# Convolution taps summed in a PSUM bank, and a front norm with its GpSimd work taken out or moved, in the second block's mixer

## The chip, the cores and the metric

The kernel runs on one NeuronCore of a Trainium2 chip. The engines are TensorE (PE in the profile), VectorE (DVE), ScalarE (ACT), GpSimd (POOL) and SyncE (SP, which only issues DMAs). The metric is the device time in microseconds, and the median of several runs stands for a kernel.

## The reference, cut to what matters

A network of four layers comes first (two gated units, a recurrence and an attention), then a second block, to which the change belongs. Its mixer computes:

```python
proj = u @ w_in + b_in                       # u: 512 tokens, 1024 features, normed and modulated
q, f, i, og, ca, cgt = split(proj)           # six parts of 512 columns
o = hgrn2(q, f, i)                           # a gated recurrence, 4 heads of 128
h_a = o * rsqrt(mean(o*o)) * norm_w * silu(og)
a = ca * sigmoid(cgt)
a = causal depthwise conv of a, 31 taps for each of the 512 channels, + conv_b
h_b = silu(layernorm(a) * conv_g + conv_bb)
y = concat(h_a, h_b) @ w_out + b_out
```

Behind it stand a residual with a norm, and a mixture of 16 experts of which each token takes two.

## The kernel before, in words

All matrix products are made of three: weights and activations are split into a high half (ScalarE casts, `whi`) and a low half (VectorE subtracts, `wlo`, line 164), and `mm3` (line 171) multiplies high by high, high by low and low by high. A weight block of 128 x 1024 is 24 such matmuls for all 512 tokens. `split()` (line 2838) turns the oldest loaded block into halves and issues the next load; one block is split ahead.

Block 2 (`block2`, line 2811) is issued under a manual schedule: each engine works its instructions strictly in the order in which the program writes them, and waits only for data and for buffers. The names that follow are those of the profile.

- **Front norm**, lines 2854 to 2923. `bn_aggr` gives mean and variance of each token, `col_bcast` (line 275) turns them across into a PSUM bank (`mean`, later `rb`), and `rstd_steps` (line 256) makes the inverse root in 13 small VectorE steps (`ln_x`, `ln_t`, `ln_y`). Before the root, ScalarE copies `mean` to SBUF (`ms`), GpSimd subtracts it from feature chunks 5, 6, 7 (`HSG`, line 2870) and then adds the output bias `b2_gb` to the four token tiles `xtok` (line 2872), which are used only at the end of the block. VectorE subtracts `mean` from chunks 0 and 1 between its root's steps (`HSN`). Then, chunk by chunk, VectorE multiplies by `rb` (`h_make`), ScalarE applies the modulation and makes the high half (`h_split`; for the chunks of `HXV` VectorE does one of the two), VectorE makes the low half (`h_lo`), and TensorE multiplies two blocks with the chunk.
- **Projections.** `proj` makes one block of 128 columns, `projt` the forget gate (`fb`) and the input gate (`ib`) with the tokens on the partitions, four weight blocks each. `fpost` (line 3040) is the chain of elementwise steps behind the forget gate; `steps` (line 3074) issues a step of it and taps behind each half block of `projt(ib)`, and goes on into `rest` (q, the second half of the convolution's inputs, the output gate) for `NPRE` = 14 steps.
- **Convolution.** `taps` (line 2973) is a generator with one step for each of 31 taps. Channel groups 3 and 2 (`CPOOL`) have ScalarE multiply and GpSimd add (line 2982); groups 0 and 1 are one `scalar_tensor_tensor` a tap on VectorE (line 2984), which reads and writes `cv` in SBUF. `some(n)` (line 2989) issues n taps of each of the two queues. The groups enter in the order of `CONV` = 3, 0, 2, 1.
- **Heads.** `rounds` (line 3209) issues, round by round, one step of each of four heads, of the convolution's norm `cnorm` (which waits for all four groups) and of the first output products, then two steps of `rest` with one tap of each queue. At the end `out_mm` makes eight products of 512 columns, one PSUM bank each.
- **PSUM** has eight banks; the pool `ps` hands out all eight, in this block and in the experts behind it (`moe`, line 3564).

Of the kernel before, what the change touches and what calls it, by code (L numbers as in the profile page):

```python
# [26 lines left out]
F32 = mybir.dt.float32  # L27
# [3 lines left out]
OP = mybir.AluOpType  # L31
AX = mybir.AxisListType
P = 128
D = 1024
KC = 8
# [33 lines left out]
CPOOL = (2, 3)  # L69
CONV = (3, 0, 2, 1)  # L70
NTMP = 4
NPRE = 14
NC0 = 2
NT0 = 1
NT1 = 1
# [3 lines left out]
YP = (0, 2, 4)  # L79
# [11 lines left out]
MXV = ((), ())  # L91
MLG = ((), ())
MHA = 2
HSG = (5,6,7)
HSN = (6,10)
HSP = 1
HXV = (1, 3, 5, 7)
HLG = ()
HA = 2
NRAW = 13  # L100
# [20 lines left out]
class Net:  # L121
# [23 lines left out]

    def psum(self, name="ps"):
        return self.ps.tile([P, 512], F32, name=name, tag="ps", bufs=self.nps)

    def psum2(self, name="ps2"):
        return self.ps.tile([P, 1024], F32, name=name, tag="ps2", bufs=self.nps2)  # L150
# [43 lines left out]
    def v(self, name, i=0, n=1):  # L194
        o = VEC[name][0] + i
        return self.vec[:, o:o + n]
# [2614 lines left out]
    def block2(self):  # L2811
        nc, A, v = self.nc, self.A, self.v
        V, S, G, MM = nc.vector, nc.scalar, nc.gpsimd, nc.tensor.matmul
        T = TX
# [17 lines left out]
        bst, bp, xtok, g1 = self.b2st, self.b2p, self.x1, self.b2_g1  # L2832
# [5 lines left out]
        def split(eng=None):  # L2838
            if raws:
                W.append(self.wsplit2(raws.pop(0), eng=eng))  # L2840
                load()
# [3 lines left out]
        def tl(name, shape, bufs=1, dt=F32, pool=bp):  # L2845
            return pool.tile(list(shape), dt, name="b_" + name, bufs=bufs)
# [9 lines left out]
        mv = tl("mv", (P, 4, 2))  # L2856
        for t in range(4):
            V.bn_aggr(mv[:, t, :], self.b2_st[:, t])
        mean = self.col_bcast(mv[:, :, 0], 4)[0]
        rstd = self.rstd_steps(bp, mv[:, :, 1], 4, 1.0, 1e-5, "ln1")  # L2860
        xs = [x[:, :T] for x in self.xT]
        xst, xp = self.open("b2x")
        hst, hp = self.open("b2h")
        tri = tl("tri", (P, 2, P))
        nc.sync.dma_start(tri, A["b2_tri"])
        if HSG:
            ms = tl("ms", (P, T), 1, F32, hp)
            S.copy(ms, mean)
        for c in HSG:
            G.tensor_tensor(xs[c], xs[c], ms, op=OP.subtract)  # L2870
        for t in range(4):
            G.tensor_tensor(xtok[t], xtok[t], self.b2_gb, op=OP.add)
        subs = [c for c in range(KC) if c not in HSG]
        for n, r in enumerate(rstd):
            if n in HSN:
                c = subs.pop(0)
                V.tensor_tensor(xs[c], xs[c], mean, op=OP.subtract)
        rb = self.col_bcast(r, 4)[0]
        h = [tl("h", (P, 2, T), KC, F32R, xp) for _ in range(KC)]

        def h_make(c):
            if c in subs:
                V.tensor_tensor(xs[c], xs[c], mean, op=OP.subtract)
            V.tensor_tensor(xs[c], xs[c], rb, op=OP.mult)

        def h_split(c):
            x, b, w = xs[c], mod[:, c, 0:1], mod[:, KC + c, 0:1]
            S.activation(h[c][:, 0, :], x, AF.Identity, bias=b, scale=w)
            if c in HXV:
                V.tensor_scalar(x, x, w, b, op0=OP.mult, op1=OP.add)  # L2890
            else:
                S.activation(x, x, AF.Identity, bias=b, scale=w)

        def h_lo(c):
            (G if c in HLG else V).tensor_tensor(h[c][:, 1, :], xs[c], h[c][:, 0, :], op=OP.subtract)

        def projt(banks):

            for k2 in range(4):
                hi, lo = W.pop(0)  # L2900
                for t in range(4):
                    tk = slice(t * P, (t + 1) * P)
                    for kk in range(2):
                        k = 2 * k2 + kk
                        ws = slice(kk * 512, (kk + 1) * 512)
                        self.mm3(banks[t], h[k][:, 0, tk], h[k][:, 1, tk], hi[:, ws], lo[:, ws], k == 0, k == KC - 1)
                    if t == 1:
                        split()
                    if t % 2:
                        yield  # L2910
# [5 lines left out]
        for k in range(KC):  # L2916
            h_split(k)
            if k + HA < KC:
                h_make(k + HA)
            h_lo(k)  # L2920
            ks = slice(k * P, (k + 1) * P)
            for n in range(2):
                self.mm3(first2[n], W[n][0][:, ks], W[n][1][:, ks], h[k][:, 0, :], h[k][:, 1, :], k == 0, k == KC - 1)
        del W[:2]
        split()
        hb = tl("hb", (P, 24))
# [6 lines left out]
        hst, hp = self.open("b2h2")  # L2933
# [3 lines left out]
        ap_ = [tl("apad", (P, 30 + T), 4, F32, wo) for _ in range(4)]  # L2937
        cv = [tl("cv", (P, T), 4, F32, wo) for _ in range(4)]
# [34 lines left out]
        def taps(c):  # L2973
            for j in range(31):
                w = v("b2_cw", 4 * j + c)
                if j == 0:
                    E = G if c in CPOOL else V
                    E.tensor_scalar(cv[c], ap_[c][:, 0:T], w, v("b2_cb", c), op0=OP.mult, op1=OP.add)
                elif c in CPOOL:
                    pt_ = tl("ctap", (P, T), 2, F32, hp)  # L2980
                    S.activation(pt_, ap_[c][:, j:j + T], AF.Copy, scale=w)
                    G.tensor_tensor(cv[c], cv[c], pt_, op=OP.add)
                else:
                    V.scalar_tensor_tensor(cv[c], ap_[c][:, j:j + T], w, cv[c], op0=OP.mult, op1=OP.add)
                yield

        todo, done = {0: [], 1: []}, []

        def some(n):
            for q in todo.values():  # L2990
                m = n
                while m > 0 and q:
                    if next(q[0], q) is q:
                        done.append(q.pop(0))
                    m -= 1

        def convs(c):
            ca = tmp("ca")

            def first(ps):  # L3000
                S.activation(ca, ps, AF.Identity, scale=0.5, bias=hb[:, 16 + c:17 + c])

            def second(ps):
                gated(ap_[c][:, 30:], ps, 20 + c, ca)
                todo[c in CPOOL].append(taps(c))

            return first, second

        def rest():
            for c in range(4):  # L3010
                yield from proj(lambda ps, c=c: gated(qf[c], ps, c, None))
            for c in conv[NC0:]:
                for then in convs(c):
                    yield from proj(then)
            for c in range(4):
                yield from proj(lambda ps, c=c: gated(og[c], ps, 12 + c, None))
            while late:
                late.pop(0)()
# [7 lines left out]
        fb, ib = ([self.psum() for _ in range(4)] for _ in range(2))  # L3026
# [44 lines left out]

        fpo = fpost()

        def steps(it, n=99):
            for _ in itertools.islice(it, n):
                next(fpo, None)
                some(NT1)

        next(fpo)
        next(fpo)  # L3080
        steps(projt(ib))
        for t in range(4):
            V.tensor_tensor(vt[t], ib[t], bi, op=OP.add)
        re = rest()
        steps(re, NPRE)
        for _ in fpo:
            pass
        fst.close()
# [3 lines left out]
        So, Wo, YP = {}, {}, {}  # L3092
# [165 lines left out]
        def out_mm(t, n, ks):  # L3258
            tk, ns = slice(t * P, (t + 1) * P), slice(n * 512, (n + 1) * 512)
            if (t, n) not in YP:  # L3260
                YP[t, n] = self.psum()
            for k in ks:
                self.mm3(YP[t, n], So[k][:, 0, tk], So[k][:, 1, tk], Wo[k][0][:, ns], Wo[k][1][:, ns], k == 4, k == 3)

        def early():

            for _ in range(WS):
                yield
            rest_done()
            for k in (4, 5):  # L3270
                wout(k, [self.wp.tile([P, UW], F32R, name=n, tag=n, bufs=2) for n in ("whi", "wlo")], (V, G)[WE[k - 4]])
                yield
            while 6 not in So:
                yield
            for t, n in EARLY:
                out_mm(t, n, (4, 5))
                yield
# [12 lines left out]
        ost, op = self.open("b2o")  # L3290
        for k in (6, 7, 0, 1, 2, 3):
            t = tl("wo", (P, 2, D), 6, F32R, op)
# [20 lines left out]
        def out_all():  # L3313
            for t in range(4):
                for n in range(2):
                    out_mm(t, n, (6, 7, 0, 1, 2, 3) if (t, n) in YP else (4, 5, 6, 7, 0, 1, 2, 3))
# [726 lines left out]
```

## Time and profile before

| what | value |
| --- | --- |
| median of 3 runs | 3743.05 us (3726.38 to 3746.35) |
| the profiled execution | 3755.24 us, span 3753.5 us |
| TensorE busy | 3339.8 us, 89% |
| VectorE busy | 2440.1 us, 65% |
| ScalarE busy | 1687.9 us, 45% |
| GpSimd busy | 1261.2 us, 34% |
| mean granted clock of TensorE | 0.917 |

The profile is of one execution; times in its rows count from the start of its span. [...] The idle time ahead of an instruction stands in brackets with what ended it. Block 2's mixer lies between some 2948 and 3270 us, the experts from 3375 to 3690.

### The profile page before, as it was taken

The numbers are of one execution on the slowest core, as the hardware profiler recorded it, in microseconds if no ns is written. First come the engines' busy times: TensorE is split into PE (matmuls) and PEld (weight loads), VectorE is DVE, ScalarE is ACT, GpSimd is POOL, SyncE is SP. The second block draws the span as 40 slices with busy tenths as digits, with TensorE's granted clock in tenths as the row PEclk, the third lists the DMA queues.
The fourth block names the chain that finished last, engine by engine and source line by source line (L and its number), as shares of the span: only waits on it lengthen the run. The fifth ranks groups of instructions, "written<-read, shape, count | busy, mean of one in ns | idle before, by whom it ended". The sixth has DMA issues, their size and how long they took to land. (4 is left out here: it accounts for less than half of the span.)

```text
span 3753.5 us, 63762 instructions
## 1 busy us (share of the span) xinstructions
PE 3339.8 (89%) x24742; PEld 2822.9 (75%) x24742; DVE 2440.1 (65%) x4326; ACT 1687.9 (45%) x2853; POOL 1261.2 (34%) x1542
## 2 busy tenths in 40 slices
PE   7999998989588988988999998899999879769993
PEld 4788887768477788776878887787788658658882
DVE  6777777453576766646435555546675687789995
ACT  3322223433354645555336666543223455327872
POOL 0031002220256766730023424300210348326664
PEclk8999998989787978799999999999999889769996
DMA  5443453246864444454432222244662211149982
GB/s 219 145 144 133 144 202 105 70 162 188 249 190 141 125 141 135 121 179 133 138 104 55 68 63 66 84 145 154 205 216 98 77 66 39 61 165 363 387 334 96
DMA packets 349426, 554.46 MB, mean 148 GB/s; under 512 B 170561, under 2 KB 225985, under 8 KB 349121
## 3 DMA queue, kind: packets, MB, share of 16 engines
q1 hardware_dynamic: 345520, 537.25, 43.7%
q0 software_dynamic: 3600, 13.11, 1.0%
q8 instruction: 196, 3.21, 0.4%
q14 instruction: 110, 0.89, 0.1%
HBM read 451.42 MB, written 88.36 MB: 144 GB/s over the span
## 5 line engine op out<-in xcount | busy, mean ns | idle before, releaser
L164 DVE TENSOR_TENSOR wlo<-wraw,whi 128x1024 fp32r<-128x1024 f32 x220 | 288.3, 1311 | 175.4 <-ACT whi L163 162.9
L163 ACT CAST whi<-wraw 128x1024 fp32r<-128x1024 f32 x221 | 231.5, 1047 | 312.9 <-PE ps L174 183.4
L173 PE MATMUL ps<-hl,whi 128*128 128x512 f32 (+1 forms) x992 | 363.3, 366 | 1.6 <-ACT hl L1954 1.6
L175 PE MATMUL ps<-hl,wlo 128*128 128x512 f32 (+1 forms) x992 | 359.9, 363 | 2.5 <-DVE wlo L164 2.5
L174 PE MATMUL ps<-hl,whi 128*128 128x512 f32 (+1 forms) x992 | 360.2, 363 | 1.5 <-DVE hl L1959 1.5
L3629 ACT CAST e_wsp<-mraw 128x1024 fp32r<-128x1024 f32 x189 | 197.3, 1052 | 56.2 <-PE ps L175 32.0
L175 PEld LDWEIGHTS ps<-hl,wlo 128*128 128x128 f32 x992 | 188.6, 190 | 33.9 <-DVE wlo L164 3.7
L174 PEld LDWEIGHTS ps<-hl,whi 128*128 128x128 f32 x992 | 188.7, 190 | 33.7 <-DVE hl L1959 4.9
L173 PEld LDWEIGHTS ps<-hl,whi 128*128 128x128 f32 x992 | 188.5, 190 | 30.8 <-ACT hl L1954 2.0
L3630 POOL TENSOR_TENSOR e_wsp<-mraw,e_wsp 128x1024 fp32r<-128x1024 f32 x63 | 164.7, 2614 | 131.2 <-ACT e_wsp L3629 60.5
L3630 DVE TENSOR_TENSOR e_wsp<-mraw,e_wsp 128x1024 fp32r<-128x1024 f32 x126 | 183.8, 1493 | 24.1 <-ACT e_wsp L3629 23.8
L1531 POOL TENSOR_TENSOR s_tmp<-s_N,s_P 128x15 f32<-128x15 f32 (+4 forms) x360 | 127.9, 355 | 147.3 <-DVE s_N L1515 109.8
L209 DVE SCALAR_TENSOR_TENSOR araw<-araw,conds 128x1024 f32<-128x1024 f32 x128 | 157.0, 1231 | 25.0 <-DMA araw<-ada 24.1
L626 POOL TENSOR_SCALAR v<-v,vr_y 128x256 f32<-128x256 f32 x70 | 93.1, 1348 | 158.8 <-DVE vr_y L272 158.8
L173 PE MATMUL ps<-whi,hl 128*128 128x512 f32 x320 | 131.0, 409 | 8.8 <-ACT hl L406 7.1
L173 PE MATMUL ps<-s,whi 128*128 128x512 f32 (+1 forms) x384 | 138.6, 361 | 0.0
L175 PE MATMUL ps<-s,wlo 128*128 128x512 f32 (+1 forms) x384 | 137.1, 357 | 0.2 <-DVE wlo L164 0.2
L174 PE MATMUL ps<-s,whi 128*128 128x512 f32 (+1 forms) x384 | 137.2, 357 | 0.0
L169 DVE TENSOR_TENSOR a_pt<-ps,a_pt 128x512 fp32r<-128x512 f32 (+1 forms) x128 | 69.1, 553 | 102.3 <-ACT a_pt L168 102.3
L174 PE MATMUL ps<-wlo,hl 128*128 128x512 f32 x320 | 130.7, 408 | 4.9 <-DVE wlo L164 4.9
L175 PE MATMUL ps<-whi,hl 128*128 128x512 f32 x320 | 130.2, 407 | 0.9 <-DVE hl L413 0.8
L1532 POOL TENSOR_TENSOR s_P<-s_P,s_tmp 128x15 f32<-128x15 f32 (+4 forms) x360 | 120.7, 335 | 28.2
(963 smaller groups left out, 10091.6 us busy)
## 6 DMA issues: line engine op xcount, KB each, us to landing
mraw<-moe_w SPq DMA_DIRECT2D x192, 512.0 KB, 6.5
araw<-ada SPq DMA_DIRECT2D x136, 512.0 KB, 3.9
wraw<-sgu_v SPq DMA_DIRECT2D x40, 512.0 KB, 4.0
wraw<-rw_in SPq DMA_DIRECT2D x40, 512.0 KB, 5.4
d_n<-ff SPq DMA_DIRECT2D x48, 384.0 KB, 5.3
s_fn<-d_n SPq DMA_DIRECT2D x24, 768.0 KB, 5.9
wraw<-sgu_out SPq DMA_DIRECT2D x34, 512.0 KB, 4.4
wraw<-sgu_u SPq DMA_DIRECT2D x32, 512.0 KB, 4.6
```

The source lines that it names most:

```text
L163: self.nc.scalar.copy(hi[:, :cols], t[:, :cols])
L164: (eng or self.nc.vector).tensor_tensor(lo[:, :cols], t[:, :cols], hi[:, :cols], op=OP.subtract)
L169: (eng or self.nc.vector).tensor_tensor(lo, src, hi, op=OP.subtract)
L173: mm(out, lh, rh, start=start, stop=False)
L174: mm(out, lh, rl, start=False, stop=False)
L175: mm(out, ll, rh, start=False, stop=stop)
L209: self.nc.vector.scalar_tensor_tensor(junk, w, 0.5, c, op0=OP.mult, op1=OP.mult, accum_out=out)
L626: e.tensor_scalar(vt[g][:, t, :], vt[g][:, t, :], r[:, t:t + 1], None, op0=OP.mult)
L1531: TTG(o, N[:, None, ts, s].to_broadcast([P, nj, nt]), Pm[:, js, s:s + 1].to_broadcast([P, nj, nt]), op=OP.mult)
L1532: TTG(Pm[:, js, ts], Pm[:, js, ts], o, op=OP.subtract)
L3629: S.copy(hl[:, 0, :], raw)
L3630: (G if j % 3 == 2 else V).tensor_tensor(hl[:, 1, :], raw, hl[:, 0, :], op=OP.subtract)
```

## The change

The settings `HSG` and `HSN` go, and `HXV` becomes empty: all eight chunks are subtracted by VectorE behind the root, two of them (`HA`) ahead of the first product, and ScalarE does both modulations of each chunk. The four additions of `b2_gb` are written behind the loop of the first two projections. The pool of PSUM is closed and opened again with seven banks; the eighth is `acc`, in which VectorE's taps of a group add up, and from which ScalarE copies the sum to `cv` behind the last tap. `projt(ib)` issues no taps (`steps(projt(ib), 0)`). The last of the eight output products takes the bank `acc`.

```diff
-HSG = (5,6,7)
-HSN = (6,10)
-HXV = (1, 3, 5, 7)
+HXV = ()
...
+    def acc(self):
+        return self.ps.tile([P, 512], F32, name="acc", tag="acc", bufs=1)
...
             V.bn_aggr(mv[:, t, :], self.b2_st[:, t])
+        self.pst.close()
+        self.open_psum(7, 0)
         mean = self.col_bcast(mv[:, :, 0], 4)[0]
...
-        if HSG:
-            ms = tl("ms", (P, T), 1, F32, hp)
-            S.copy(ms, mean)
-        for c in HSG:
-            G.tensor_tensor(xs[c], xs[c], ms, op=OP.subtract)
-        for t in range(4):
-            G.tensor_tensor(xtok[t], xtok[t], self.b2_gb, op=OP.add)
-        subs = [c for c in range(KC) if c not in HSG]
-        for n, r in enumerate(rstd):
-            if n in HSN:
-                c = subs.pop(0)
-                V.tensor_tensor(xs[c], xs[c], mean, op=OP.subtract)
+        subs = list(range(KC))
+        for r in rstd:
+            pass
         rb = self.col_bcast(r, 4)[0]
+        for _ in range(HA):
+            c = subs.pop(0)
+            V.tensor_tensor(xs[c], xs[c], mean, op=OP.subtract)
...
                 self.mm3(first2[n], W[n][0][:, ks], W[n][1][:, ks], h[k][:, 0, :], h[k][:, 1, :], k == 0, k == KC - 1)
+        for t in range(4):
+            G.tensor_tensor(xtok[t], xtok[t], self.b2_gb, op=OP.add)
...
-                    E.tensor_scalar(cv[c], ap_[c][:, 0:T], w, v("b2_cb", c), op0=OP.mult, op1=OP.add)
+                    acc = cv[c] if c in CPOOL else self.acc()
+                    E.tensor_scalar(acc, ap_[c][:, 0:T], w, v("b2_cb", c), op0=OP.mult, op1=OP.add)
...
-                    G.tensor_tensor(cv[c], cv[c], pt_, op=OP.add)
+                    G.tensor_tensor(acc, acc, pt_, op=OP.add)
                 else:
-                    V.scalar_tensor_tensor(cv[c], ap_[c][:, j:j + T], w, cv[c], op0=OP.mult, op1=OP.add)
+                    V.scalar_tensor_tensor(acc, ap_[c][:, j:j + T], w, acc, op0=OP.mult, op1=OP.add)
                 yield
+            if c not in CPOOL:
+                S.copy(cv[c], acc)
...
-        def steps(it, n=99):
-            for _ in itertools.islice(it, n):
+        def steps(it, n, m=99):
+            for _ in itertools.islice(it, m):
                 next(fpo, None)
-                some(NT1)
+                some(n)
...
-        steps(projt(ib))
+        steps(projt(ib), 0)
...
-        steps(re, NPRE)
+        steps(re, NT1, NPRE)
...
-                YP[t, n] = self.psum()
+                YP[t, n] = self.acc() if (t, n) == (3, 1) else self.psum()
```

## Rows read from the trace of the kernel before

**Rows 1.** Stretches: us, busy us (instructions) of each engine, TensorE's clock, DMA share, GB/s
```profile
2991.00:3013.00 22.00, 22.00 (x96) 17.73 (x95) 18.22 (x13) 12.59 (x18) 15.40 (x10) 1.00 0.35 115
3013.00:3078.00 65.00, 39.52 (x146) 29.83 (x145) 60.80 (x64) 33.45 (x47) 29.02 (x19) 0.82 0.14 45
3078.00:3112.00 34.00, 34.00 (x175) 27.53 (x174) 14.44 (x18) 16.31 (x26) 6.42 (x5) 1.00 0.25 84
...
3160.00:3190.00 30.00, 24.73 (x167) 22.69 (x166) 29.79 (x30) 14.50 (x24) 29.53 (x25) 0.94 0.05 18
3190.00:3204.00 14.00, 11.06 (x80) 10.71 (x81) 13.86 (x17) 3.32 (x6) 12.27 (x12) 0.88 0.01 1
3375.00:3650.00 275.00, 270.40 (x1331) 223.66 (x1330) 257.63 (x279) 219.09 (x257) 176.03 (x72) 1.00 0.97 371
```

**Rows 2.** Waits of TensorE, 2948 to 3250: us in total, times, longest
```profile
PE ps L174 <- DVE wlo L164: 12.6, 3, 6.6
PE ps L175 <- DVE wlo L164: 10.6, 2, 10.1
```

**Rows 3.** Timeline at the front norm: start us, us, engine, line, operation
```profile
2946.27 2.34 POOL L164 TENSOR_TENSOR wlo<-wraw,whi 128x1024 fp32r<-128x1024 f32 x1 [60.18 <-ACT whi L163]
...
2946.97 2.06 ACT L2767 ACTIVATE b_xtok<-ps 128x512 f32<-128x512 f32 x4 [0.78 <-DVE b_st L2764]
...
2949.30 0.16 DVE L270 TENSOR_TENSOR ln_t<-ln_t,ln_x 128x4 f32<-128x4 f32 x1
...
2949.75 3.71 POOL L2870 TENSOR_TENSOR xT<-xT,b_ms 128x512 f32<-128x512 f32 x3 [1.14 <-ACT b_ms L2868]
...
2952.29 1.19 DVE L268 TENSOR_TENSOR ln_t<-ln_y 128x4 f32<-128x4 f32 x1
2953.41 9.26 POOL L2872 TENSOR_TENSOR b_xtok<-b_xtok,b_gb 128x1024 f32<-128x1024 f32 x4
2953.51 2.26 DVE L270 TENSOR_TENSOR ln_t<-ln_t,ln_x 128x4 f32<-128x4 f32 x1
2955.69 0.67 DVE L2877 TENSOR_TENSOR xT<-xT,ps 128x512 f32<-128x512 f32 x1
2956.29 1.78 DVE L272 SCALAR_TENSOR_TENSOR ln_y<-ln_t,ln_y 128x4 f32<-128x4 f32 x1
```

**Rows 4.** Taps and line 744, each from its line's view: ns min/median/max
```profile
L2984 DVE SCALAR_TENSOR_TENSOR b_cv<-b_apad,vec,b_cv x60: 729/1218/1849, 2996.9 to 3203.5; 128x512 f32<-128x512 f32 x60
...
L2982 POOL TENSOR_TENSOR b_cv<-b_cv,b_ctap x60: 1264/1594/2300, 2982.8 to 3189.5; 128x512 f32<-128x512 f32 x60
...
L744 DVE TENSOR_TENSOR ps<-ps,f x6: 690/699/700, 596.8 to 618.8; 128x512 f32<-128x512 f32 x6
```

**Rows 5.** Timeline of VectorE, 2990 to 3075 us
```profile
3009.93 3.49 DVE L2984 SCALAR_TENSOR_TENSOR b_cv<-b_apad,vec,b_cv 128x512 f32<-128x512 f32 x2
...
3020.35 1.23 DVE L164 TENSOR_TENSOR wlo<-wraw,whi 128x1024 fp32r<-128x1024 f32 x1 [1.63 <-ACT whi L163]
...
3031.99 2.29 DVE L164 TENSOR_TENSOR wlo<-wraw,whi 128x1024 fp32r<-128x1024 f32 x1
...
3046.82 1.21 DVE L164 TENSOR_TENSOR wlo<-wraw,whi 128x1024 fp32r<-128x1024 f32 x1
3047.95 0.68 DVE L3059 TENSOR_TENSOR b_fab<-b_fab,b_omlb 128x512 f32<-128x512 f32 x1
...
3051.18 0.43 DVE L3061 TENSOR_SCALAR b_fab<-b_fab 128x512 f32<-128x512 f32 x1
...
3069.08 2.28 DVE L164 TENSOR_TENSOR wlo<-wraw,whi 128x1024 fp32r<-128x1024 f32 x1
```

**Rows 6.** Line 3067 on GpSimd, from its line's view: ns min/median/max
```profile
L3067 POOL TENSOR_TENSOR b_kt<-b_kt,b_omlb x4: 1453/1704/1764, 3039.4 to 3044.2; 128x512 f32<-128x512 f32 x4
```

**Rows 7.** Timeline of TensorE behind its longest wait
```profile
3071.41 0.80 PE L175 MATMUL ps<-b_h,wlo 128*128 128x512 f32 x1 [10.08 <-DVE wlo L164]
```

**Rows 8.** Groups by line, 3375 to 3650: busy us, mean ns | idle
```profile
L3630 DVE TENSOR_TENSOR e_wsp<-mraw,e_wsp 128x1024 fp32r<-128x1024 f32 x114 | 168.7, 1517 | 9.9 <-ACT e_wsp L3629 9.6
```

## The prediction

> **What bounds the kernel now.** I read the table of stretches first, because the change touches only the second block's mixer (2948 to some 3270 us of the span) and one average over 3753 us says nothing of it. In [rows 1] a projection runs with TensorE always busy: 96 matmuls in 22.00 us, so 0.23 us each at a granted clock of 1.00. The next row is the weak place: from 3013 to 3078 us TensorE gets through 146 matmuls, which at that pace are 34 us, and takes 65. VectorE is busy 60.8 of these 65. That stretch is the projection of the input gate (`projt(ib)`) with the forget gate's chain `fpost` beside it, and the first two blocks of `rest`. From 3160 to 3204 VectorE and GpSimd are both full (29.79 and 29.53 of 30 in its first row) or nearly, and TensorE idles 5.3 and 2.9 us.
>
> The waits of TensorE then name who is late. [rows 2]: 12.6 + 10.6 us for the low half of a weight (`wlo`, line 164), which VectorE makes in its program order. So the bound from 3013 to 3078 is not VectorE's work as such, but what is queued on VectorE ahead of each `wlo`. Everything in block 2 hangs on the step before it, so time won there shifts all behind it, the prefetch of the experts' weights too, which is issued by the same order.
>
> **The front norm** (lines 2856 to 2885). What the reader is to see in [rows 3] is the pairing: a step of the root's chain that needs 0.16 us takes 1.19 us beside a 1.24 us GpSimd subtraction and 2.26 us beside a 2.3 us addition of `b2_gb` (four in 9.26 us): while GpSimd works, one VectorE step with two SBUF operands gets through per GpSimd instruction. The subtraction that reads `mean` from PSUM is not held (0.67 us). The chain of 13 steps ends at 2958.07 instead of some 2.6 us after 2948.5.
>
> The change takes the three GpSimd subtractions and the copy `ms` away and writes the four additions behind the first projection loop. But they are moved past no GpSimd instruction: nothing in that loop is on GpSimd. What they need is there early: GpSimd has finished its `wlo` at 2946.27 + 2.34 = 2948.6, ScalarE the copies to `xtok` at 2949.0 [rows 3]. GpSimd works its own queue in order and has nothing else to wait for, so I expect them to run from 2948.7 to 2958.0, **earlier** than now, on top of the root's chain. Four steps pass in these 9.3 us, eight or nine are left at 0.2 us: `ln_y` at 2959 to 2959.7, that is 0.9 to 1.6 us later than now. Behind it VectorE has 22 instructions for h (8 products, 6 subtractions, 8 low halves) against 23 now (it gets three subtractions, and loses four `tensor_scalar` to ScalarE). I take **1 us lost** for the front, with bounds from 7 won (additions truly late: 2958.07 - 2951.1) to 2 lost.
>
> **A tap's price.** [rows 4]: 60 taps of VectorE take 0.729 us at least, 1.218 in the median, 1.849 at most. With the sum in PSUM a tap has one SBUF operand, as the subtraction of `mean` in [rows 3] that was not held, and the one form of this trace that reads and writes a PSUM bank on VectorE (line 744, as wide) takes 0.699. I take 0.73. GpSimd's additions of taps (1.264 least, 1.594 median) lose their hindrance too. [...]
>
> **The input gate's projection.** Now 8 taps of VectorE and 8 of ScalarE and GpSimd are issued in it; after, none. I follow the ends of the low halves in [rows 5], since each releases the next 24 matmuls (5.6 us).
> - Two taps ahead of `fpost` (3009.93, 3.49 us) become 1.5: the low half that ends at 3021.6 ends at 3019.7.
> - Next (3034.3 now): four of line 3050, four of lines 3054 and 3055, the low half, all at their price without GpSimd (0.65 each, 1.23), and 0.7 of waiting: 7.0 us, so 3026.7.
> - Next (3048.0 now): four of lines 3054 and 3055, six of lines 3059 to 3061 (3047.95 to 3051.6, so 3.6 us for six), the low half: 7.5. GpSimd's products for `kt` remain (line 3067, [rows 6], four of 1.7) and now fall here: in some 6.5 us four steps get through where nine would, 3.7 us lost (0 to 5). So 3037.8. TensorE waits here 5.5 us.
> - [...] I take 7.4 us in place of 5.6, to 3045.2.
> - The block after it waits for the four sums of line 3070, four of `vt`, one tap and a low half, 3051.4, where it is 3071.4 now [rows 5].
>
> That is **20 us won**; between 15 (GpSimd holds VectorE more than I think) and 25 (the `kt` products cost nothing).
>
> **Where the moved taps go.** VectorE's eight end up in the first rounds of the heads, where it is busy 14.44 of 34 us [rows 1]: nothing. GpSimd's 14 or so now stand beside the projections of q, four to a 5.6 us block at 1.27 us and ScalarE's whole share, with the weights' casts behind them on ScalarE: GpSimd needs nearly as long as TensorE. I take 2 us lost (0 to 5). No tap becomes due later: the second convolution channel of each engine is queued only when its projection is through, after the first is done in both kernels.
>
> **The heads.** From 3160 to 3190 GpSimd makes some 12 additions; at 0.33 us less, 4 us. From 3190 to 3204 VectorE alone is the bound, 9 taps at half a microsecond less, of which TensorE's idle 2.9 us allows 2. Together **6 us won** (0 to 8.2, TensorE's idle there). The two new copies from PSUM stand on ScalarE behind the last tap: 1 us lost (0 to 2).
>
> **The sum:** -1 + 20 - 2 + 6 - 1 = 22 us. The profiled execution took 3755.2 us (span 3753.5), so 3733 by it; the median of the runs is 3743.05, 12 us below, and 22 us less is **3721 us**.
>
> **Rivals.**
> (a) The additions do run behind the norm, as the change's words have it: front 7 won in place of 1 lost, 3713. For it: the words. Against: no wait that I can find.
> (b) The stretch of `ib` is held by the chain of `fpost` itself (ScalarE's Exp and Ln and its table loads between VectorE's steps) and by `kt`, and GpSimd bounds the heads: 10 won there, 0 in the heads, some 9 in all, 3734. For it: ScalarE waits for VectorE and the reverse in turn. Against: VectorE is busy 60.8 of 65, so it hardly waits.
> (c) **Slower**: one of the eight PSUM banks is taken out of the pool for good, as the pool is not opened again; the experts (3375 to 3650) use eight banks a round: gate, up, turned h, two of turned u, the slots' list, two of down. TensorE is busy 270.4 of 275 there [rows 1], so any wait counts. If the second bank of down had to wait for the gelu that frees the gate's bank, it would stand behind VectorE's two weight splits, 2 x 1.52 us [rows 8], in 15 experts: 46 us, 3767. From 1.5 us an expert it decides. Against: at that point only four tiles are live, and the three other banks were read long before. [...]
> (d) `kt` costs nothing and the heads give all of TensorE's idle time: 33 won, 3710.
>
> **How the numbers follow.** My forecast 0.52 (3713 to 3730), (a) 0.12, (b) 0.22, (c) 0.06, (d) 0.08. The range takes in (a), (b), (d) and the spread of the bounds, 3705 to 3739, and leaves out (c) and the far ends. About 0.5% (18.7 us) is what can be told from no change: the forecast's own bounds lie two thirds beyond it; with (a) and (d) faster 0.55, same 0.38, slower 0.07.
>
> **What would show it.** GpSimd's four additions start before 2949 us, not behind the first projection; the root's chain still has steps of over 2 us. Taps at 0.70 to 0.75 everywhere. From 3013 TensorE's waits for `wlo` sum to under 10 us instead of 23, the largest at the fourth block of `ib`. From the first heads to the last tap, TensorE no longer idles some 8 us. From 3375 on nothing but a shift. The forecast is wrong if the additions are late, if the waits for `wlo` stay, or if TensorE shows new waits in the experts.

## The result and the profile after

The changed kernel takes **3721.24 us** in the median of 20 runs, the kernel before 3744.14 us (20 runs). The ratio is **0.9942 with a 95% interval from 0.993 to 0.9954**, so 17 to 26 us faster. The forecast was 3721.

The profiled execution of the changed kernel took 3714.86 us (span 3713.1), 40.4 us less than that of before. That is not all due to the change. The aggregation of the front norm (`bn_aggr`) is the last instruction ahead of the first changed one, and it starts at 2947.85 us before and at 2935.82 after, though both kernels issue the same instructions up to there. In the profiles of the experiments below, all alike up to that point, it starts anywhere between 2929.09 and 2958.20. So every time of block 2 is given here from the **start of that aggregation** in the same profile. How good this ruler is, the run with seven banks shows: it has the same instructions in the same order as the kernel before, and its 22 low halves and the norm's first matmul stand within 0.1 us of those of before.

| us after the aggregation's start | before | after | won so far |
|---|---|---|---|
| transposes of `ln_y` | 10.3 | 11.4 | -1.1 |
| first low half behind the first projection, end | 30.65 | 31.06 | -0.4 |
| input gate's stretch, first low half, end | 73.73 | 72.50 | 1.2 |
| second | 86.43 | 79.95 | 6.5 |
| third | 100.18 | 91.54 | 8.6 |
| fourth | 107.56 | 97.97 | 9.6 |
| fifth | 123.51 | 106.50 | 17.0 |
| fourth low half behind these (just past the projections of q) | 147.37 | 129.55 | 17.8 |
| two further, in the first rounds of the heads | 165.00 | 146.85 | 18.15 |
| last tap of VectorE, end | 256.41 | 230.93 | 25.5 |
| first matmul of the convolution's norm | 258.01 | 233.82 | **24.2** |

From the norm's first matmul to the first cast of the experts' weights by line 3629 (three such casts of another line come earlier) it is 157.8 us before and 152.7 after; the same stretch lies between 152.8 and 157.7 us in the twelve other kernels. From that cast to the last it is 317.3 us before and 318.4 after, and from there to the end 72.5 and 72.4.

The 5 us behind the norm are a matter of TensorE's clock. The 20 us that begin 50 us behind the norm's first matmul, before and after (columns as in [rows 1]):

```profile
3255.86:3275.86 20.00, 18.52 (x66) 15.49 (x66) 7.34 (x6) 4.13 (x7) 2.77 (x1) 0.58 0.53 176
3219.64:3239.64 20.00, 18.53 (x85) 14.93 (x85) 11.07 (x13) 4.15 (x7) 2.77 (x1) 0.84 0.52 176
```

TensorE is busy for the same 18.5 us, but gets through 66 matmuls at a granted clock of 0.58 (0.50 for the first 16.94 us, then 1.00) and 85 at 0.84 (0.50 for 6.54 us in two pieces, 1.00 for the rest). Its waits just ahead are alike, some 4.0 and 1.6 us for a weight `b_wo`. Whether the change brings this or the moment does stays open: the traces of kernels that hold the change lie on both sides.

The clock has a part in the 24.2 us too. From the aggregation to the norm, before and after:

```profile
2947.85:3205.86 258.01, 210.91 (x1100) 176.06 (x1101) 205.39 (x222) 128.27 (x191) 161.07 (x121) 0.90 0.16 54
2935.82:3169.64 233.82, 206.05 (x1101) 171.79 (x1101) 168.55 (x221) 131.91 (x196) 143.51 (x118) 0.94 0.18 59
```

TensorE's idle time falls by 19.3 us (47.1 to 27.8), and the same matmuls take 4.9 us less at a granted clock of 0.94 instead of 0.90. (The run with seven banks, with the instructions of before, has 45.8 us idle and 212.1 busy; so the split is good to some 1.3 us.)

The stretches of the changed kernel that answer to [rows 1] (us, busy us and instructions of TensorE, its weight loads, VectorE, ScalarE, GpSimd; TensorE's granted clock, DMA share, GB/s):

```profile
2979.00:3001.00 22.00, 22.00 (x97) 17.74 (x95) 12.74 (x15) 12.95 (x18) 14.60 (x10) 1.00 0.35 117
3001.00:3049.00 48.00, 38.78 (x152) 29.39 (x151) 42.81 (x53) 30.27 (x43) 18.38 (x12) 0.93 0.17 56
...
3042.00:3064.00 22.00, 21.58 (x100) 16.87 (x101) 20.33 (x24) 16.33 (x25) 18.91 (x12) 1.00 0.35 117
...
3130.00:3160.00 30.00, 25.54 (x182) 23.45 (x181) 21.55 (x32) 14.51 (x24) 25.93 (x28) 0.97 0.01 1
...
3335.00:3610.00 275.00, 271.16 (x1324) 224.64 (x1322) 254.94 (x279) 218.18 (x255) 176.07 (x72) 0.99 0.96 370
```

The second row is the stretch that took 65 us in [rows 1] for 146 matmuls at a granted clock of 0.82; now 152 matmuls take 48 us at 0.93. TensorE's idle time in it falls from 25.5 to 9.2 us, though VectorE is still busy 42.8 of 48. The experts' row is as it was.

TensorE's waits in block 2's mixer after the change, the answer to [rows 2] (us in total, times, longest):

```profile
PE ps L282 <- DVE ln_y L273: 10.4, 1, 10.4
PE ps L282 <- DVE hr_y L273: 8.8, 4, 2.9
PE ps L175 <- DVE wlo L165: 7.8, 3, 5.7
...
PE ps L3168 <- POOL g_x L3162: 2.6, 3, 1.2
PE ps L176 <- DVE wlo L165: 1.9, 2, 1.4
PE ps L3168 <- POOL g_x L3163: 1.9, 1, 1.9
```

The waits for `wlo` (line 165 here) are 9.7 us instead of 23.2. The longest wait of all is now the one for the root's chain. In the heads, up to the last tap, TensorE now waits for GpSimd alone (the two rows with `g_x`, 4.5 us); the waits for `hr_y`, the root of the heads' own norm, come behind it. Before, most of the wait there was for VectorE:

```profile
PE ps L3166 <- DVE g_x L3161: 5.8, 3, 3.7
PE ps L3166 <- POOL g_x L3161: 2.4, 1, 2.4
```

VectorE's taps in their bank and GpSimd's additions, from their lines' views (ns min/median/max), stand against [rows 4]:

```profile
L2984 DVE SCALAR_TENSOR_TENSOR acc<-b_apad,vec,acc x60: 731/750/756, 2984.8 to 3166.0; 128x512 f32<-128x512 f32 x60
```

```profile
L2982 POOL TENSOR_TENSOR b_cv<-b_cv,b_ctap x60: 1267/1308/2180, 2971.2 to 3155.2; 128x512 f32<-128x512 f32 x60
```

All 60 taps of VectorE lie within 25 ns of each other, whatever GpSimd does beside them, and GpSimd's median falls from 1.594 to 1.308 us.

GpSimd at the front norm, answering to [rows 3]:

```profile
2934.24 2.35 POOL L165 TENSOR_TENSOR wlo<-wraw,whi 128x1024 fp32r<-128x1024 f32 x1 [60.23 <-ACT whi L164]
2936.55 9.22 POOL L2922 TENSOR_TENSOR b_xtok<-b_xtok,b_gb 128x1024 f32<-128x1024 f32 x4
```

and the root's steps on VectorE, from the second to the seventh of 13:

```profile
2936.67 2.24 DVE L263 TENSOR_SCALAR ln_t<-ln_x 128x4 int32<-128x4 int32 x1
2938.95 2.26 DVE L265 TENSOR_SCALAR ln_y<-ln_t 128x4 int32<-128x4 int32 x1
2941.12 0.16 DVE L266 TENSOR_SCALAR ln_x<-ln_x 128x4 f32<-128x4 f32 x1
2941.24 2.25 DVE L269 TENSOR_TENSOR ln_t<-ln_y 128x4 f32<-128x4 f32 x1
2943.53 2.26 DVE L271 TENSOR_TENSOR ln_t<-ln_t,ln_x 128x4 f32<-128x4 f32 x1
2945.82 0.16 DVE L273 SCALAR_TENSOR_TENSOR ln_y<-ln_t,ln_y 128x4 f32<-128x4 f32 x1
```

The four additions are written behind the first projection, but GpSimd has nothing in between to wait for: they start the moment its `wlo` is done, on top of the chain. Each of the four costs the chain one step of 2.25 us; all later steps take 0.16.

The input gate's stretch on VectorE, its five low halves and the four sums of line 3072 ahead of the last one, answering to [rows 5]:

```profile
3007.09 1.23 DVE L165 TENSOR_TENSOR wlo<-wraw,whi 128x1024 fp32r<-128x1024 f32 x1 [1.63 <-ACT whi L164]
...
3014.55 1.22 DVE L165 TENSOR_TENSOR wlo<-wraw,whi 128x1024 fp32r<-128x1024 f32 x1
...
3026.14 1.22 DVE L165 TENSOR_TENSOR wlo<-wraw,whi 128x1024 fp32r<-128x1024 f32 x1
...
3032.56 1.23 DVE L165 TENSOR_TENSOR wlo<-wraw,whi 128x1024 fp32r<-128x1024 f32 x1 [1.63 <-ACT whi L164]
3033.70 3.60 DVE L3072 TENSOR_TENSOR b_g<-b_g,b_fab 128x512 f32<-128x512 f32 x4
...
3040.28 2.04 DVE L165 TENSOR_TENSOR wlo<-wraw,whi 128x1024 fp32r<-128x1024 f32 x1
```

and TensorE's waits in it, answering to [rows 7]:

```profile
3008.37 0.50 PE L175 MATMUL ps<-wlo,b_h 128*128 128x512 f32 x1 [0.77 <-DVE wlo L165]
3015.82 0.50 PE L175 MATMUL ps<-wlo,b_h 128*128 128x512 f32 x1 [1.30 <-DVE wlo L165]
3027.41 0.80 PE L175 MATMUL ps<-wlo,b_h 128*128 128x512 f32 x1 [5.72 <-DVE wlo L165]
3042.38 0.50 PE L176 MATMUL ps<-b_h,wlo 128*128 128x512 f32 x1 [1.37 <-DVE wlo L165]
```

One wait of 5.72 us is left, at the third low half, which feeds the input gate's fourth block. Between the second and the third low half (3015.77 to 3027.36) GpSimd makes its products for `kt`, from 3015.61 to 3023.42.

### The profile page after: what moved, and what is told of

It reads as the page before. It is cut to its first block, busy times and chain, and to the rows that moved or that the text cites. A ratio compares the mean times of both kernels' runs of the same rounds, so it can differ in the third digit from the quotient of the medians.

```text
span 3713.1 us, 63753 instructions
## 1 busy us (share of the span) xinstructions
PE 3324.1 (90%) x24742; PEld 2811.4 (76%) x24742; DVE 2401.3 (65%) x4325; ACT 1692.7 (46%) x2858; POOL 1244.6 (34%) x1539
## 5 line engine op out<-in xcount | busy, mean ns | idle before, releaser
L210 DVE SCALAR_TENSOR_TENSOR araw<-araw,conds 128x1024 f32<-128x1024 f32 x128 | 157.7, 1236 | 25.4 <-DMA araw<-ada 24.8
L175 PE MATMUL ps<-wlo,hl 128*128 128x512 f32 x320 | 129.5, 405 | 4.9 <-DVE wlo L165 4.9
```

Of the source, the lines that this page charges most:

```text
L175: mm(out, lh, rl, start=False, stop=False)
L210: self.nc.vector.scalar_tensor_tensor(junk, w, 0.5, c, op0=OP.mult, op1=OP.mult, accum_out=out)
```

## The experiments

In what follows "third" and "fifth" are the ends of those low halves of the input gate's stretch, "norm" the first matmul of the convolution's norm, all from the aggregation's start; the ratio is that of the times against the kernel before, with its 95% interval. For comparison: before 100.18, 123.51, 258.01; with the change 91.54, 106.50, 233.82. The whole times scatter by 5 to 30 us between runs of one kernel, so where two kernels differ by less than some 8 us it is the trace that tells them apart.

### The taps stay beside the input gate, the sums go to PSUM

```diff
-        steps(projt(ib), 0)
+        steps(projt(ib), NT1)
```

> The changed kernel with one tap of each engine issued again at every step of the input gate's projection; the sums stay in PSUM, the front stays as changed. From the end of the aggregation of the front norm to the last low half of the input gate it was 123.5 us before and 106.5 with the change. My theory: VectorE gets some 8 taps back at 0.75 us (6 us) and GpSimd some 8 additions, each of which lets one two-operand SBUF step of VectorE through at 1.2 instead of 0.65 us (some 5 us): that point at 117 us; the projections of q and the heads win 2 us back, so some 13 us faster than the kernel before (ratio 0.9965). Rival, the PSUM sum alone does it: that point at 109 us at most, 20 us faster than before. Rival, taking the taps out does it all and PSUM nothing: that point at 121 us or later, 6 us faster or less.

Measured: third 97.96, fifth 118.05, norm 247.53; ratio 0.9969 (0.9952 to 0.9986), 12 us faster than before. The fifth low half came 1 us behind my figure. The 2 us that should come back behind it did not: from the fifth low half to the norm it is 129.5 us against 127.3. The PSUM bank alone (with the front as changed) is worth 10.5 us of the 24.2.

### No taps beside the input gate, the sums stay in SBUF

```diff
-                    acc = cv[c] if c in CPOOL else self.acc()
+                    acc = cv[c]
-            if c not in CPOOL:
-                S.copy(cv[c], acc)
```

> The changed kernel with VectorE's sums in SBUF as before (no accumulator bank in use by the taps, no copies); no taps beside the input gate. My theory: the input gate comes out nearly as with the change (last low half 108 us after the aggregation, against 106.5; the taps ahead of it in the forget gate's projection are 2 us longer), and the heads lose their 6 us again, the projections of q 1 to 2: 14 us faster than the kernel before (ratio 0.9963). Rival, the PSUM sum alone does it: 3 to 5 us faster than before. Rival, taking the taps out does it all: 20 us or more faster.

Measured: third 93.16, fifth 108.97, norm 249.73; ratio 0.9988 (0.9973 to 1.0003). By the trace 8.3 us are won, where I expected 14; the whole time hardly shows a gain. The input gate came as expected (108). The miss is behind it: from the fifth low half to the fourth one after it, through the projections of q, this kernel takes 30.4 us and the changed one 23.05, so 7.4 us are lost where I had put 1 to 2; the heads then lose 6.1. VectorE in two of those projections:

```profile
3070.09 5.18 DVE L2984 SCALAR_TENSOR_TENSOR b_cv<-b_apad,vec,b_cv 128x512 f32<-128x512 f32 x3
3075.20 1.77 DVE L2970 SCALAR_TENSOR_TENSOR b_qf<-tt 128x512 f32<-128x512 f32 x1
...
3078.70 5.14 DVE L2984 SCALAR_TENSOR_TENSOR b_cv<-b_apad,vec,b_cv 128x512 f32<-128x512 f32 x3
```

Three taps take 5.14 us (1.71 each) beside GpSimd's additions; with the low half and the gate's product a projection takes 8.6 us of VectorE, where TensorE needs 5.6. So moving the taps pays only if they are also short in the new place. That is why the two halves together (24.2) are worth more than their sum (10.5 + 8.3).

### Seven PSUM banks in the kernel before

```diff
+        self.pst.close()
+        self.open_psum(7, 0)
...
-                YP[t, n] = self.psum()
+                YP[t, n] = self.acc() if (t, n) == (3, 1) else self.psum()
```

> The kernel before, with nothing changed but the PSUM pool: from the front norm of the second block on it has seven banks, and the eighth serves one tile of the output projection only. My theory: nothing to see, within 3 us of the kernel before; the experts' stretch as long as before within 1 us. Rival (c) of the prediction, the experts wait for the seventh bank: 46 us slower (ratio 1.012), with new waits of TensorE in every expert. In between (5 to 20 us slower): the heads or the experts wait now and then.

Measured: third 100.17, fifth 123.49, norm 257.92; ratio 0.9998 (0.9981 to 1.0016). Nothing moves, in block 2 nor in the experts, whose row reads

```profile
3367.00:3642.00 275.00, 271.39 (x1343) 225.03 (x1342) 259.81 (x281) 220.15 (x259) 178.60 (x72) 1.00 0.97 371
```

against 270.40 us of TensorE in 275 in [rows 1]. Rival (c) falls.

### kt without GpSimd's products

```diff
-                V.tensor_tensor(x, ls, x, op=OP.subtract)
                 V.tensor_tensor(ls, ls, l1, op=OP.add)
+                V.tensor_tensor(x, ls, x, op=OP.subtract)
...
-                G.tensor_tensor(kt[t], x, omlb, op=OP.mult)
```

> The changed kernel without GpSimd's four products for kt: the factor 1 - lb goes into the exponent (the sum with its logarithm is made ahead of the difference, by the same two VectorE steps in the other order), so kt comes out of the Exp as it is. My theory: the 3.7 us that these products hold VectorE beside the input gate are won: its third low half comes 3 to 4 us earlier (91.5 us after the aggregation with the change, 88 here), and all behind it; 26 to 27 us faster than the kernel before (ratio 0.993). Rival (d) of the prediction, the products cost nothing: third low half at 91 us, 23 us faster than before. Rival, more than one VectorE step is held per product: 30 us faster.

Measured: third 87.97, fifth 105.81, norm 233.00; ratio 0.9942 (0.9921 to 0.9964), as with the change. The third low half comes 3.57 us earlier, which is the 3.7 us of the prediction. At the fifth only 0.7 of it is left. VectorE there:

```profile
3038.36 1.23 DVE L165 TENSOR_TENSOR wlo<-wraw,whi 128x1024 fp32r<-128x1024 f32 x1 [1.64 <-ACT whi L164]
3039.50 6.89 DVE L3071 TENSOR_TENSOR b_g<-b_g,b_fab 128x512 f32<-128x512 f32 x4
```

and GpSimd:

```profile
3039.09 6.75 POOL L2982 TENSOR_TENSOR b_cv<-b_cv,b_ctap 128x512 f32<-128x512 f32 x4 [28.81 <-ACT b_ctap L2981]
```

The four sums take 6.89 us instead of 3.60: GpSimd's first taps behind the input gate now start together with them, and each of the four holds one sum for 1.7 us. The time was won and given back at the next place where the two engines meet.

### The additions truly late

```diff
                 G.tensor_tensor(kh[t], kh[t], kt[t], op=OP.mult)
+                G.tensor_tensor(xtok[t], xtok[t], self.b2_gb, op=OP.add)
```

(and the loop of additions behind the first projection goes)

> The changed kernel with GpSimd's four additions of b2_gb written behind the four products for kh (one behind each), some 130 us later, where GpSimd and VectorE have room. My theory: the root's chain is not held, its transposes start 3 us after the start of the aggregation instead of 11.4, the low half behind the first projection loop ends at 23 instead of 31.1, and the 8 us stay to the end: 31 us faster than the kernel before (ratio 0.9918). Rival: the time is given back, because the 9.2 us of GpSimd then stand in front of the first taps and products of the heads: the first matmul of the convolution's norm at 231 us or later (233.8 with the change), 23 to 26 us faster than before.

Measured: transposes of `ln_y` at 3.05, first low half behind the first projection 22.73, third 83.18, fifth 97.31, norm 223.14; ratio 0.9921 (0.99 to 0.9942), median 3713.18 us, 30 us faster than before. Of the root's chain nothing is held now (two of its steps):

```profile
2937.19 0.17 DVE L263 TENSOR_SCALAR ln_t<-ln_x 128x4 int32<-128x4 int32 x1
...
2939.17 0.16 DVE L273 SCALAR_TENSOR_TENSOR ln_y<-ln_t,ln_y 128x4 f32<-128x4 f32 x1
```

The 8.3 us stay to the end and grow to 10.7. So what still held the root's chain in the changed kernel is GpSimd's additions and nothing else, and rival (a) had the right price (8 us between it and the forecast) but not the right kernel.

### kt without products, and no taps while the sums are made

```diff
-        steps(re, NT1, NPRE)
+        steps(re, 0, 4)
+        steps(re, NT1, NPRE - 4)
+        some(4)
```

(on top of kt without GpSimd's products)

> The kernel with kt out of the exponent, and in it no taps at the first four steps behind the input gate (the block of the first projection of q); four of each engine are issued at the end instead. The run with kt alone won 3.6 us at the third low half and gave 2.9 back at the fifth, since GpSimd's taps started at once and fell on VectorE's four sums (6.89 us in place of 3.60). My theory: without taps there the sums take 2.6 us, the fifth low half ends at 101 to 102 instead of 105.8, the projections of q end 4.5 us earlier than with the change, and the later taps cost 1 to 3 of it: 2 to 4 us faster than the change, 26 us faster than the kernel before (ratio 0.993). Rival, the taps of GpSimd bound the heads: nothing is left, 20 us or less faster than before.

Measured: third 87.96, fifth 100.34, norm 230.50; ratio 0.9922 (0.9899 to 0.9945), 29 us faster than before. The four sums take their own time:

```profile
3030.68 2.49 DVE L3071 TENSOR_TENSOR b_g<-b_g,b_fab 128x512 f32<-128x512 f32 x4
...
3062.69 1.13 DVE L2970 SCALAR_TENSOR_TENSOR b_qf<-tt 128x512 f32<-128x512 f32 x1 [3.20 <-ACT tt L2969]
```

So the giving back of the run before is confirmed: without GpSimd at that place the fifth low half is 6.2 us earlier than with the change. Of that 3.3 are left at the norm. The second line shows one place where it goes: ScalarE stands behind the four taps that were put at the end, and VectorE waits 3.20 us for it.

### All three

Additions behind the products for `kh`, `kt` out of the exponent, no taps in the first projection of q, four at the end.

> Both together: the additions behind the products for kh, kt out of the exponent, no taps in the block of the first projection of q. My theory: the two gains add up, 8 and 2 to 4 us, 34 us faster than the kernel before (ratio 0.991). Rival: GpSimd, which gets 9.2 us of additions and four taps just ahead of the heads, is late there: 28 us or less.

Measured: fifth 92.00, norm 223.78; ratio 0.9907 (0.9886 to 0.9928), median 3710.76 us, 35 us faster than before by the whole time. By the trace the two gains do not add: 34.2 us are won at the norm, 0.6 less than with the late additions alone. The block that follows the four taps at the end is late: its low half ends at 122.41, 13.05 us after the one before it, where the blocks ahead are 6.7 us apart.

### All three without the taps at the end

```diff
-        some(4)
```

> The kernel with all three (additions behind the products for kh, kt out of the exponent, no taps in the block of the first projection of q), without the four taps of each engine that were issued at the end of the projections of q. In the run with them the sixth projection's low half came 6.4 us late (122.4 us after the aggregation, where 109.4 + 6.7 was due), since ScalarE stood behind those taps. My theory: it comes at 116, and the first matmul of the convolution's norm at 219 to 221 instead of 223.8, since GpSimd has four taps more in the heads: 3707 us, 36 us faster than the kernel before (ratio 0.9903). Rival, the taps left over bound the heads: 223 or later, 31 us or less.

Measured: fifth 91.97, the low half in question 118.40 (116 expected; it takes 2.74 us instead of 1.22, beside one of the additions of `b2_gb`), norm 220.09; ratio **0.9898 (0.9881 to 0.9915)**, median 3709.54 us. By the trace 37.9 us are won against the kernel before and 13.7 against the change.

### All three, the additions ahead of the first taps

```diff
             G.memset(ap_[c][:, :30], 0.0)
+        for t in range(4):
+            G.tensor_tensor(xtok[t], xtok[t], self.b2_gb, op=OP.add)
```

(in place of the additions behind the products for `kh`)

> The same with GpSimd's four additions behind the memsets of the convolution's padding instead of the products for kh: the memsets wait for the last low halves of h, so the additions run behind the root's chain, ahead of the first taps. My theory: the chain ends as early as with the additions far behind (3 us after the aggregation's start), the first low half behind the first projection takes 2.3 instead of 1.2 us and costs TensorE 1 us, and GpSimd is free for the left taps: first matmul of the convolution's norm at 218 to 221, 36 to 38 us faster than the kernel before (ratio 0.990). Rival: the additions delay GpSimd's first taps and these the heads; 223 or later.

Measured: transposes of `ln_y` at 3.04, first low half behind the first projection 23.74, the next 30.04 (26.34 with the additions far behind), fifth 94.29, norm 219.76; ratio **0.9904 (0.9888 to 0.9919)**, median 3707.48 us. The memsets wait for VectorE's low halves of h (12.46 us ahead of the first memset), which come behind the chain, and this keeps the additions off it. The 2.3 us that the additions cost the projections are made up in the heads. The two versions can't be told apart; both beat the changed kernel.

### VectorE's second channel in SBUF again

```diff
-                    acc = cv[c] if c in CPOOL else self.acc()
+                    acc = cv[c] if c != 0 else self.acc()
```

> The changed kernel with the sums of VectorE's second channel alone (c = 1, its taps run in the heads) in SBUF as before; the first channel's stay in PSUM. My theory: the projections come out as with the change, and the heads lose the 6 to 7 us that they won: first matmul of the convolution's norm at 240 us after the aggregation instead of 233.8, 16 us faster than the kernel before. Rival, the heads were won by the taps' new place or by GpSimd alone: 236 at most.

Measured: third 91.52, fifth 106.46, the fourth low half behind the fifth 129.63 (129.55 with the change), norm 239.99; ratio 0.9942 (0.9927 to 0.9957). Up to the heads it is the changed kernel; the heads lose 6.2 us, as expected. The whole time does not resolve this. In the heads TensorE now waits 5.0 us for VectorE's product `g_x`, a wait that the kernel before has (5.8 us) and the changed kernel does not:

```profile
PE ps L3168 <- DVE g_x L3163: 5.0, 2, 3.4
PE ps L3168 <- POOL g_x L3163: 2.4, 1, 2.4
```

### One engine's taps beside the input gate

GpSimd's and ScalarE's alone:

```diff
-        steps(projt(ib), 0)
+        steps(projt(ib), NT1, 99, (1,))
```

> The changed kernel with GpSimd's and ScalarE's taps alone issued again beside the input gate, VectorE's not. With both the last low half of the input gate's stretch came at 118.05 us after the aggregation, with none at 106.5. My theory: of these 11.5 us VectorE's own eight taps are 6 and the steps that GpSimd holds 5 to 6: 112 us here. Rival, the hindrance is all: 116 or later. Rival, only VectorE's own work counts: 108 at most.

VectorE's alone:

```diff
-        steps(projt(ib), 0)
+        steps(projt(ib), NT1, 99, (0,))
```

> The changed kernel with VectorE's taps alone issued again beside the input gate, GpSimd's and ScalarE's not. GpSimd's alone put the last low half of that stretch from 106.5 to 114.6 us after the aggregation, both together to 118.05. If the two add up: 110 us here (3.4 us more than with none). My theory, their own durations: eight taps at 0.75 us, 112.5. Rival: VectorE has idle time for them, 108 at most.

Measured with GpSimd's: third 96.19, fifth 114.62, norm 244.14; ratio 0.9946 (0.9925 to 0.9966). With VectorE's: third 93.41, fifth 108.99, norm 236.56; ratio 0.9941 (0.9926 to 0.9957). So of the 11.55 us that both cost at the fifth low half GpSimd's additions cost 8.1 and VectorE's own taps 2.5 (the rest, 0.9, only both together); I had 5.5 and 6. VectorE's eight taps, 0.75 us each, are 6 us of work. Part of it fits where VectorE waits in the changed kernel, 1.63 us for ScalarE ahead of the fourth low half; with VectorE's taps ahead of it that wait is

```profile
3040.88 1.23 DVE L165 TENSOR_TENSOR wlo<-wraw,whi 128x1024 fp32r<-128x1024 f32 x1 [0.18 <-ACT whi L164]
```

The rest of the difference was not followed up. GpSimd's work holds VectorE's steps: GpSimd and VectorE in the run with GpSimd's taps,

```profile
3045.26 1.30 POOL L2982 TENSOR_TENSOR b_cv<-b_cv,b_ctap 128x512 f32<-128x512 f32 x1 [2.57 <-ACT b_ctap L2981]
3046.52 6.46 POOL L3069 TENSOR_TENSOR b_kt<-b_kt,b_omlb 128x512 f32<-128x512 f32 x4
...
3045.27 1.84 DVE L3062 TENSOR_TENSOR b_fab<-b_fab,b_lb 128x512 f32<-128x512 f32 x1
3047.14 1.37 DVE L3063 TENSOR_SCALAR b_fab<-b_fab 128x512 f32<-128x512 f32 x1
...
3055.03 0.69 DVE L3062 TENSOR_TENSOR b_fab<-b_fab,b_lb 128x512 f32<-128x512 f32 x1
3055.76 0.43 DVE L3063 TENSOR_SCALAR b_fab<-b_fab 128x512 f32<-128x512 f32 x1
```

The same steps take 1.84 us beside a tap and 1.37 beside a product for `kt`, and 0.69 and 0.43 with GpSimd idle: some 1 us lost for each instruction of GpSimd. Up to the fifth low half this run has eight taps of GpSimd more than the changed kernel (12 against 4), which at 1 us each is the 8.1 us.

## Why the prediction was right

The time was right, and so was the mechanism behind the larger part of it; two terms of the sum were off in opposite directions. That the median (3721.24) falls on the forecast to 0.2 us is luck: the interval of the gain is 9 us wide, the trace gives 24.2 us where the sum has 22, and single terms are off by up to 3 us.

| term | forecast | measured by the trace |
|---|---|---|
| front | -1 | -1.1 at the root's chain, -0.4 at the next low half |
| input gate's stretch | +20 | +17.4 |
| moved taps of GpSimd beside the q projections | -2 | +1.1 (17.0 won at the fifth low half, 18.15 in the first rounds) |
| heads | +6 | +7.3 (25.5 won at the last tap) |
| copies of the sums | -1 | -1.3 |
| sum | 22 | 24.2; 22 by the whole times (17 to 26) |

- **The front.** The step held: GpSimd's additions are moved past none of its instructions, so they start earlier, at 2936.55, 0.7 us after the aggregation. The chain's end moves 1.1 us (0.9 to 1.6 forecast). The run with the additions late shows that the chain's 8.3 us hang on nothing else. The forecast's count of 22 instructions leaves out the two subtractions ahead of the first product (1.28 us together); they ran while TensorE turned the root. What the moved subtractions and modulations are worth by themselves no run shows.
- **A tap's price.** Forecast 0.73, measured 0.731 to 0.756, with a median of 0.750. The 0.729 of [rows 4] is the least of 60; the 15 taps of the kernel before that no instruction of GpSimd overlaps took 0.740 to 0.752, with a median of 0.747, one of them being

```profile
3046.16 0.74 DVE L2984 SCALAR_TENSOR_TENSOR b_cv<-b_apad,vec,b_cv 128x512 f32<-128x512 f32 x1
```

So the sum in PSUM costs the tap nothing that these rows show (0.003 us). A tap with its sum in PSUM took 0.756 us at most, whatever GpSimd did beside it, while one with it in SBUF is held: a median of 0.750 against 1.638 in the run with the sums in SBUF. The TENSOR_SCALAR steps in the last section, with one SBUF input as these taps, are held all the same (1.37 us against 0.43); what sets them apart no run shows.
- **The input gate's stretch.** With the 0.4 us of the front taken off, the first, second, third and fifth low halves come 0.3, 0.7, 1.2 and 2.5 us later than forecast. The forecast's fourth figure (3045.2) is the end of TensorE's block, not of a low half: from the end of its wait that block took 7.4 us, as forecast, and added nothing. No row of before shows the 7.4 us that the sum takes there in place of 5.6; in the changed kernel the 23 matmuls behind the wait of 5.72 us took 7.37 us, nine of them 3.99 at a granted clock of 0.50 and the rest 3.38 at 0.97. The 3.7 us for `kt` were good (3.57 when taken away). The step that failed is the last: "the four sums of line 3070, four of `vt`, one tap and a low half". I put all of these at their unhindered price, though GpSimd's moved taps start just there: the sums take 3.60 us instead of 2.5, the low half 2.04 instead of 1.22. These 1.9 us cover the 1.3 that this step adds of its own.
- **The q projections.** The hindrance of GpSimd's moved taps that I had put here, 2 us, is the one that fell on the fifth low half. In the projections themselves VectorE's low halves run ahead of TensorE, which is busy 21.58 of the 22 us from 3042 to 3064, and a little more is won. The two terms together are 18.5 us where 18 were forecast: the cost was there, one step earlier.
- **The heads.** 7.3 us, 6 forecast, up to the last tap; over the same matmuls up to the norm, with the copies, 6.0 are won, 3.7 of them idle time of TensorE (8.2 to 4.5) and 2.3 its clock (0.96 to 0.98), a part that the forecast did not count. That VectorE's taps in PSUM carry it, and not the place of the taps, the run with the second channel in SBUF shows (6.2 us). Of the signs that I named, one failed: TensorE still idles 4.5 us there, for GpSimd.
- **The rivals.** (a) falls by the first row of GpSimd; its 8 us were real, but for a kernel that was not this one. (b), 10 us with nothing in the heads, falls by both terms; ScalarE's table loads in that chain, which it names, are four of 1.28 us each in the trace of before. (c) falls by the run with seven banks: the norm's first matmul came at 257.92 us against 258.01, and TensorE was busy 271.39 us of the experts' 275 against 270.40. (d) had `kt` free: it is not, though taking it away brings nothing by itself. Its price was also mis-added: 25 and 8.2 with the sum's three losses are 29 us, not 33.

What I had not priced well is the share of the two engines beside the input gate: in the expectations VectorE's own taps and the steps that GpSimd holds were about equal, and the runs gave GpSimd three quarters (8.1 of 10.6 us). The sum didn't suffer, since the change moves both.

Left open: whether the 5 us that TensorE's clock gives behind the norm belong to the change.

## What to carry to other kernels

When an instruction of GpSimd is written later, look for what it will wait for: without a wait between the old place and the new one it runs earlier, not later (here 0.7 us after the aggregation's start in place of 5.56). Moving work off a full stretch pays by what the work costs in its new place, so ask first whether it is short there (here: a sum in PSUM instead of SBUF, 0.750 us a tap against 1.638), and look for the next place where the moved instructions meet the other engine (here four sums, 6.89 us in place of 3.60). Where upstream scatter is larger than the change, compare traces from the last common instruction.

## What the runs showed of the hardware

- Steps of VectorE with a single SBUF operand are held too: a TENSOR_SCALAR of 128x4 took 2.24 and 2.26 us beside GpSimd's additions and 0.17 without, and one of 128x512 1.37 against 0.43. My prediction spoke of steps with two SBUF operands.
- Where both engines add up taps in SBUF all the time, a tap of VectorE and one of GpSimd pass every 1.7 us (5.14 us for three), where alone they take 0.75 and 1.27.
- With fewer waits TensorE's clock was higher: behind waits of 0.77 to 1.37 us the first matmul takes 0.50 us at a granted clock of 1.00, behind one of 5.72 us 0.80 at 0.50, and the same matmuls from the aggregation to the norm took 206 us at a granted clock of 0.94, with 27.8 us idle, and 211 at 0.90, with 47.1 idle.
- Two profiles of kernels with the same instructions agree within 0.1 us over the 258 us behind a common instruction, while that instruction itself scatters by 29 us of 2950 from one profile to another.
